# Short-sequence attention on one core: groups of 8 heads with wide PSUM evacuations, a three-stage order written by hand, and casting loads of 16 heads

## The chip, the core and the metric

The kernel runs on one core of a Trainium2 chip. A core has a matrix engine (PE), whose results land in PSUM (8 banks of 2 KB in each of 128 partitions), a vector engine (DVE) and an activation engine (ACT) that read PSUM and write SBUF, a general engine (POOL), a sync engine (SP) and 16 DMA engines that move data between HBM and SBUF. Each engine works through its own instructions in order and waits on semaphores for the others. Here POOL issues the loads and SP the stores. The metric is device time in microseconds (us); lower is better.

## The reference

Softmax attention for 32 batches of 12 heads, each with 128 positions of 64 values, in float32. The 384 heads are independent of each other.

```python
batch, n_heads, seq, head_dim = 32, 12, 128, 64
scale = 1.0 / np.sqrt(q.shape[-1])
scores = scale * np.matmul(q, k.transpose(0, 1, 3, 2))
scores_max = np.max(scores, axis=-1, keepdims=True)
attn = np.exp(scores - scores_max)
attn = attn / (np.sum(attn, axis=-1, keepdims=True) + 1e-8)
return np.matmul(attn, v).astype(np.float32)
```

Both kernels leave out the maximum and divide at the end: the inputs are small, so exp of the plain scores stays in range, and a column of ones beside v gives the sum of each row with the same matmul.

## The kernel before

The loop runs over the 32 batches, and a batch's 12 heads are loaded together. A head's rows lie 256 B long in HBM (64 float32), heads 32 KB apart, so a load of `q_bf` (L52), `k_bf` (L54) or `v_bf` (L57) brings 128 x 12 runs of 256 B and casts them to bf16 on the way. These casting loads are issued by POOL. `v_bf` has a 65th column that POOL sets to 1 (L56). The pool `pbf` has three buffers of each, so a load for batch b+3 waits until batch b's tile has been used.

PE transposes two heads at a time: six transposes of q (L63) and six of k (L70) in a batch, each into a PSUM tile of its own name with one buffer (`qt_ps`, `kt_ps`). ACT copies each `qt_ps` to SBUF (L68), DVE each `kt_ps` (L75). Then, for three groups of four heads: four score matmuls (L84) into `sT_ps`, one PSUM bank a head, single-buffered; one exp of ACT over 128x512 (L92) into `attnT`; and twice two output matmuls (L103) into `o_ps`, single-buffered, each pair copied out by DVE (L110). At the end of a batch DVE takes the reciprocal of the sums (L116), multiplies (L118), and SP stores 384 KB (L119).

The order of the instructions on each engine is set by the tile framework's scheduler, which mixes the transposes of the next batch into the groups of this one; waits for data and buffers are put in by the framework.

Of the kernel before, what the change touches and what calls it, by code (L numbers as in the profile page):

```python
# [1 line left out]

# [5 lines left out]


@with_exitstack
def kernel(
    ctx: ExitStack,
    tc: tile.TileContext,
    q: bass.AP,
    k: bass.AP,
    v: bass.AP,
    out: bass.AP,
):
    nc = tc.nc  # L20
    f32 = mybir.dt.float32
    bf16 = mybir.dt.bfloat16

    B, H, S, D = q.shape
    assert S == 128 and D == 64
    scale = 1.0 / (D ** 0.5)
    HT = 128 // D
    NP = H // HT
    HX = 4
    HO = 2  # L30
    BANK = 512

    qr = q.rearrange("b h s d -> b s h d")
    kr = k.rearrange("b h s d -> b s h d")
    vr = v.rearrange("b h s d -> b s h d")
    orr = out.rearrange("b h s d -> b s h d")

    singles = ctx.enter_context(tc.tile_pool(name="singles", bufs=1))
    ident = singles.tile([128, 128], bf16)
    make_identity(nc, ident)  # L40

    pbf = ctx.enter_context(tc.tile_pool(name="pbf", bufs=3))
    pt = ctx.enter_context(tc.tile_pool(name="pt", bufs=3))
    pa = ctx.enter_context(tc.tile_pool(name="pa", bufs=6))
    po = ctx.enter_context(tc.tile_pool(name="po", bufs=2))
    ps_t = ctx.enter_context(tc.tile_pool(name="ps_t", bufs=1, space=bass.MemoryType.PSUM))
    ps_s = ctx.enter_context(tc.tile_pool(name="ps_s", bufs=1, space=bass.MemoryType.PSUM))
    ps_o = ctx.enter_context(tc.tile_pool(name="ps_o", bufs=1, space=bass.MemoryType.PSUM))

    for b in range(B):  # L50
        q_bf = pbf.tile([128, H, D], bf16, tag="q_bf")
        nc.gpsimd.dma_start(out=q_bf, in_=qr[b])  # L52
        k_bf = pbf.tile([128, H, D], bf16, tag="k_bf")
        nc.gpsimd.dma_start(out=k_bf, in_=kr[b])  # L54
        v_bf = pbf.tile([128, H, D + 1], bf16, tag="v_bf")
        nc.gpsimd.memset(v_bf[:, :, D:D + 1], 1.0)  # L56
        nc.gpsimd.dma_start(out=v_bf[:, :, :D], in_=vr[b])  # L57

        qt = pt.tile([128, NP, 128], bf16, tag="qt")
        kt = pt.tile([128, NP, 128], bf16, tag="kt")  # L60
        for p in range(NP):
            qt_ps = ps_t.tile([128, 128], bf16, tag="qt_ps")
            nc.tensor.transpose(  # L63
                qt_ps,
                q_bf[:, p * HT:(p + 1) * HT, :].rearrange("a b c -> a (b c)"),
                ident,
            )
            nc.scalar.copy(qt[:, p, :], qt_ps)  # L68
            kt_ps = ps_t.tile([128, 128], bf16, tag="kt_ps")
            nc.tensor.transpose(  # L70
                kt_ps,
                k_bf[:, p * HT:(p + 1) * HT, :].rearrange("a b c -> a (b c)"),
                ident,
            )
            nc.vector.tensor_copy(kt[:, p, :], kt_ps)  # L75

        o_b = po.tile([128, H, D + 1], f32, tag="o_b")

        for g in range(H // HX):
            sT_ps = ps_s.tile([128, HX, BANK], f32, tag="sT")  # L80
            for i in range(HX):
                h = g * HX + i
                p, j = divmod(h, HT)
                nc.tensor.matmul(  # L84
                    sT_ps[:, i, :128],
                    lhsT=kt[j * D:(j + 1) * D, p, :],
                    rhs=qt[j * D:(j + 1) * D, p, :],
                    start=True,
                    stop=True,
                )  # L90
            attnT = pa.tile([128, HX, 128], bf16, tag="attnT")
            nc.scalar.activation(  # L92
                out=attnT,
                in_=sT_ps[:, :, :128],
                func=mybir.ActivationFunctionType.Exp,
                bias=0.0,
                scale=scale,
            )
            for gg in range(HX // HO):
                o_ps = ps_o.tile([128, HO, BANK], f32, tag="o_ps")  # L100
                for i in range(HO):
                    h = g * HX + gg * HO + i
                    nc.tensor.matmul(  # L103
                        o_ps[:, i, :D + 1],
                        lhsT=attnT[:, gg * HO + i, :],
                        rhs=v_bf[:, h, :],
                        start=True,
                        stop=True,
                    )
                nc.vector.tensor_copy(  # L110
                    o_b[:, g * HX + gg * HO:g * HX + (gg + 1) * HO, :],
                    o_ps[:, :, :D + 1],
                )

        recip = po.tile([128, H], f32, tag="recip")
        nc.vector.reciprocal(recip, o_b[:, :, D:D + 1])  # L116
        o_sb = po.tile([128, H, D], f32, tag="o_sb")
        nc.vector.tensor_mul(o_sb, o_b[:, :, :D], recip.to_broadcast([128, H, D]))  # L118
        nc.sync.dma_start(out=orr[b], in_=o_sb)  # L119


# [1 line left out]
_INS = ['q', 'k', 'v']  # L123
_OUTS = [((32, 12, 128, 64), 'float32')]


# [23 lines left out]
```

## Time and profile before

| | |
|---|---|
| median of 3 runs | 226.23 us (226.22 to 226.59) |
| span of the profiled execution | 224.4 us |
| instructions | 3513 |
| HBM | 37.75 MB read, 12.58 MB written, 224 GB/s over the span |
| DMA packets | 198,674, of which 198,656 are under 512 B |
| loads, POOL's queue q0 | 148,992 packets, 18.88 MB |
| stores, SP's queue q1 | 49,664 packets, 12.58 MB |
| DMA issues | 32 each of q, k, v (192 KB, 5.1 to 6.4 us to landing) and out (384 KB, 5.7 us) |

The span runs from the first to the last instruction or transfer that the profiler saw; the time of a run has a little more around it. The profiled execution's own time outside the profiler is not listed, so its span stands beside the median. PE is TensorE's matmuls, PEld its weight loads, which lie beside the matmuls. Busy shares are of the span. In the rows by line, what stands behind the first bar is busy time in us and the mean of one instruction in ns, and behind the second the idle time of that engine just before, with what ended it. Rows of waits read: who waited, for whom, us in total, how many times, the longest. A row of the windows view has the stretch, its length, the busy us and count of PE, PEld, DVE, ACT and POOL, the granted PE clock, the DMA share and the GB/s moved, counted by the size that arrives (a load's 256 B in HBM are 128 B in SBUF). Rows of a DMA queue read packets, MB, and the time that the packets took as a share of 16 engines; an engine holds several packets at once, so this goes above 100%. In POOL's timeline a row has its start, duration, line, operation, and in brackets the idle time before.

### The profile page before, as it was taken

The page shows a single profiled execution, that of the slowest core. Times are in us where ns is not written, and L with a number is a line of the kernel's source. Part 1 is how long each engine was busy: PE and PEld are TensorE (multiplying, and loading weights), DVE is VectorE, ACT ScalarE, POOL GpSimd, SP SyncE. Part 2 cuts the span into 40 slices and gives each one's busy share as a digit, 9 for nine tenths or more (in the row PEclk, how much of TensorE's full clock was granted, in tenths as well). Part 3 has the DMA queues.
Part 4 walks back from the last instruction along what each step waited for, and adds up shares of the span by engine and source line. Part 5 has one row for each costly group of instructions (what it writes and reads, how often), then busy time and mean ns, then how long its engine had stood idle before and what let it go on. Part 6 is the DMA issues. An engine that isn't in the chain of part 4 may idle for free.

```text
span 224.4 us, 3513 instructions
## 1 busy us (share of the span) xinstructions
PE 168.3 (75%) x1152; PEld 83.1 (37%) x1152; DVE 120.2 (54%) x448; ACT 99.7 (44%) x289; POOL 101.5 (45%) x134
## 2 busy tenths in 40 slices
PE   0688787788787787877787877788877778878750
PEld 0344333344333343333343333444333334333330
DVE  0264555664555564555564555565555565456652
ACT  2554545445544445444445444444444444444320
POOL 8963455534475443455443455543355534222000
DMA  7999999999999999999999999999999999999333
GB/s 50 149 156 184 148 142 140 155 148 166 151 153 161 161 159 166 148 149 141 129 151 167 146 148 134 137 154 167 149 146 144 135 150 161 142 110 134 76 69 71
DMA packets 198674, 31.69 MB, mean 141 GB/s; under 512 B 198656, under 2 KB 198656, under 8 KB 198656
## 3 DMA queue, kind: packets, MB, share of 16 engines
q0 software_dynamic: 148992, 18.88, 131.9%
q1 hardware_dynamic: 49664, 12.58, 31.0%
q8 instruction: 9, 0.15, 0.3%
q14 instruction: 9, 0.07, 0.1%
HBM read 37.75 MB, written 12.58 MB: 224 GB/s over the span
## 4 chain that ended last, share of the span: by engine, by line
PE 64%; ACT 17%; DVE 9%; issue 6%; DMA 2%; ACTq 0%; POOL 0%; POOLq 0%
PE sT_ps L84 26%; PE qt_ps L63 14%; PE o_ps L103 14%; PE kt_ps L70 11%; ACT attnT L92 9%; ACT qt L68 7%; DVE o_b L110 5%; DVE kt L75 3%; DMA q_bf<-in_q_dram 2%; DVE o_sb L118 1%; ACTq L92 0%; DVE recip L116 0%; POOL ident masks.py:197 0%; POOLq masks.py:199 0%; POOLq L134 0%
## 5 line engine op out<-in xcount | busy, mean ns | idle before, releaser
L68 ACT COPY qt<-qt_ps 128x128 bf16<-128x128 bf16 x192 | 50.4, 263 | 69.0 <-PE qt_ps L63 69.0
L75 DVE COPY kt<-kt_ps 128x128 bf16<-128x128 bf16 x192 | 42.8, 223 | 70.8 <-PE kt_ps L70 66.1
L84 PE MATMUL sT_ps<-qt,kt 64*128 64x128 bf16 x384 | 71.5, 282 | 12.2 <-ACT attnT L92 11.5
L92 ACT ACTIVATE attnT<-sT_ps 128x512 bf16<-128x512 f32 x96 | 57.3, 597 | 47.7 <-PE sT_ps L84 42.9
L63 PE MATMUL qt_ps<-ident,q_bf 128*128 128x128 bf16 x192 | 54.2, 282 | 26.8 <-ACT qt L68 21.4
L110 DVE COPY o_b<-o_ps 128x130 f32<-128x130 f32 x192 | 55.6, 289 | 29.2 <-PE o_ps L103 28.9
L103 PE MATMUL o_ps<-v_bf,attnT 128*128 128x65 bf16 x384 | 56.8, 242 | 6.1 <-DVE o_b L110 6.1
L70 PE MATMUL kt_ps<-ident,k_bf 128*128 128x128 bf16 x192 | 56.4, 294 | 5.3 <-DVE kt L75 4.5
L84 PEld LDWEIGHTS <-kt 64*128 64x128 bf16 x384 | 26.4, 101 | 61.1 <-issue 43.0
L103 PEld LDWEIGHTS <-attnT 128*128 128x128 bf16 x384 | 34.3, 120 | 34.4 <-issue 26.5
L56 POOL MEMSET v_bf<- 128x12 bf16 x32 | 5.0, 155 | 79.9 <-PE o_ps L103 79.9
L52 POOL DMA_DIRECT2D q_bf<-in_q_dram x32 | 32.6, 1020 | 10.2 <-PE qt_ps L63 8.9
L57 POOL DMA_DIRECT2D v_bf<-in_v_dram x32 | 32.6, 1018 | 9.9 <-POOL v_bf L56 9.9
L54 POOL DMA_DIRECT2D k_bf<-in_k_dram x32 | 32.8, 1025 | 1.4 <-PE kt_ps L70 1.4
L63 PEld LDWEIGHTS <-q_bf 128*128 128x128 bf16 x192 | 18.9, 113 | 31.4 <-issue 15.7
L118 DVE TENSOR_TENSOR o_sb<-o_b,recip 128x768 f32<-128x768 f32 x32 | 30.3, 948 | 0.0
L70 PEld LDWEIGHTS <-k_bf 128*128 128x128 bf16 x192 | 23.2, 121 | 8.7 <-issue 0.9
L116 DVE RECIPROCAL recip<-o_b 128x12 f32<-128x12 f32 x32 | 7.0, 219 | 0.0
L68 ACT ACT_TABLE_LOAD x1 | 1.3, 1283 | 0.7 <-PEq L134 0.7
masks.py:199 POOL TENSOR_SCALAR_AFFINE_SELECT ident<-ident 128x128 bf16<-128x128 bf16 x1 | 0.3, 305 | 0.1
masks.py:197 POOL MEMSET ident<- 128x128 bf16 x1 | 0.2, 204 | 0.3 <-POOLq L134 0.3
L134 POOL MEMSET const-float32-0.0<- 128x1 f32 x1 | 0.1, 98 | 0.2 <-issue 0.2
(3 smaller groups left out, 0.3 us busy)
## 6 DMA issues: line engine op xcount, KB each, us to landing
out_dram<-o_sb SPq DMA_DIRECT2D x32, 384.0 KB, 5.7
q_bf<-in_q_dram POOLq DMA_DIRECT2D x32, 192.0 KB, 5.9
k_bf<-in_k_dram POOLq DMA_DIRECT2D x32, 192.0 KB, 6.4
v_bf<-in_v_dram POOLq DMA_DIRECT2D x32, 192.0 KB, 5.1
```

What stands on the lines that cost most here:

```text
L52: nc.gpsimd.dma_start(out=q_bf, in_=qr[b])
L54: nc.gpsimd.dma_start(out=k_bf, in_=kr[b])
L57: nc.gpsimd.dma_start(out=v_bf[:, :, :D], in_=vr[b])
L63: nc.tensor.transpose(qt_ps, q_bf[:, p * HT:(p + 1) * HT, :].rearrange("a b c -> a (b c)"), ident,)
L68: nc.scalar.copy(qt[:, p, :], qt_ps)
L70: nc.tensor.transpose(kt_ps, k_bf[:, p * HT:(p + 1) * HT, :].rearrange("a b c -> a (b c)"), ident,)
L75: nc.vector.tensor_copy(kt[:, p, :], kt_ps)
L84: nc.tensor.matmul(sT_ps[:, i, :128], lhsT=kt[j * D:(j + 1) * D, p, :], rhs=qt[j * D:(j + 1) * D, p, :], start=True, stop=True,)
L92: nc.scalar.activation(out=attnT, in_=sT_ps[:, :, :128], func=mybir.ActivationFunctionType.Exp, bias=0.0, scale=scale,)
L103: nc.tensor.matmul(o_ps[:, i, :D + 1], lhsT=attnT[:, gg * HO + i, :], rhs=v_bf[:, h, :], start=True, stop=True,)
L110: nc.vector.tensor_copy(o_b[:, g * HX + gg * HO:g * HX + (gg + 1) * HO, :], o_ps[:, :, :D + 1],)
L118: nc.vector.tensor_mul(o_sb, o_b[:, :, :D], recip.to_broadcast([128, H, D]))
```

## The change

The batch loop is gone. The 384 heads are one list, cut into 24 chunks of 16 heads for loads and stores and into 48 groups of 8 for compute.

- **Loads.** All 72 loads are issued ahead of everything else in the program, each of 16 heads (2048 runs of 256 B), into 24 buffers of each kind, so none waits for a buffer. The ones beside v are set by DVE.
- **Stage A** of a group: eight transposes (four pairs of q and of k) into one PSUM tile `t_ps` of 1024 bf16, and one DVE copy of all of it. Two buffers.
- **Stage B**: eight score matmuls into `s_ps` (1024 float32, two banks) and one exp over 1024. Even heads lie in the first bank, odd heads in the second. Two buffers.
- **Stage C**: eight output matmuls into `o_ps` (two banks, four heads in each), one buffer; DVE takes the reciprocal and multiplies straight out of PSUM. After each second group SP stores 512 KB.
- **Order**: step s runs A of group s, B of s-1 and C of s-2, as written, not as scheduled.

```diff
-    HX = 4
-    HO = 2
-    BANK = 512
+    CH = 16
+    NCH = N // CH
+    GH = 8
+    NG = N // GH
+    GPC = CH // GH
+    HP = GH // 2
...
+    def heads(x):
+        return x.rearrange("b h s d -> s (b h) d")
...
+    pin = ctx.enter_context(tc.tile_pool(name="pin", bufs=NCH))
+    pt = ctx.enter_context(tc.tile_pool(name="pt", bufs=3))
+    pa = ctx.enter_context(tc.tile_pool(name="pa", bufs=3))
+    po = ctx.enter_context(tc.tile_pool(name="po", bufs=4))
+    ps_t = ctx.enter_context(tc.tile_pool(name="ps_t", bufs=2, space=bass.MemoryType.PSUM))
+    ps_s = ctx.enter_context(tc.tile_pool(name="ps_s", bufs=2, space=bass.MemoryType.PSUM))
+    ps_o = ctx.enter_context(tc.tile_pool(name="ps_o", bufs=1, space=bass.MemoryType.PSUM))
...
-    pbf = ctx.enter_context(tc.tile_pool(name="pbf", bufs=3))
-    pt = ctx.enter_context(tc.tile_pool(name="pt", bufs=3))
-    pa = ctx.enter_context(tc.tile_pool(name="pa", bufs=6))
-    po = ctx.enter_context(tc.tile_pool(name="po", bufs=2))
-    ps_t = ctx.enter_context(tc.tile_pool(name="ps_t", bufs=1, space=bass.MemoryType.PSUM))
-    ps_s = ctx.enter_context(tc.tile_pool(name="ps_s", bufs=1, space=bass.MemoryType.PSUM))
-    ps_o = ctx.enter_context(tc.tile_pool(name="ps_o", bufs=1, space=bass.MemoryType.PSUM))
+    chunks = {}
-    for b in range(B):
...
+    def load(c):
+        sl = slice(c * CH, (c + 1) * CH)
+        q_bf = pin.tile([128, CH, D], bf16, tag="q_bf", name="q_bf")
+        nc.gpsimd.dma_start(out=q_bf, in_=qr[:, sl, :])
+        k_bf = pin.tile([128, CH, D], bf16, tag="k_bf", name="k_bf")
+        nc.gpsimd.dma_start(out=k_bf, in_=kr[:, sl, :])
+        v_bf = pin.tile([128, CH, D + 1], bf16, tag="v_bf", name="v_bf")
+        nc.vector.memset(v_bf[:, :, D:D + 1], 1.0)
+        nc.gpsimd.dma_start(out=v_bf[:, :, :D], in_=vr[:, sl, :])
+        chunks[c] = (q_bf, k_bf, v_bf)
...
+    for c in range(NCH):
+        load(c)
...
+    with tc.manual_schedule():
+        qkts, attns, osbs = {}, {}, {}
...
+        def stage_a(i):
+            c, r = divmod(i, GPC)
+            q_bf, k_bf, v_bf = chunks[c]
+            t_ps = ps_t.tile([128, 2, HP, 128], bf16, tag="t_ps", name="t_ps")
+            for p in range(HP):
+                for j, x in enumerate((q_bf, k_bf)):
+                    h = GH * r + 2 * p
+                    nc.tensor.transpose(
+                        t_ps[:, j, p, :], x[:, h:h + 2, :].rearrange("p h d -> p (h d)"), ident)
+            qkt = pt.tile([128, 2, HP, 128], bf16, tag="qkt", name="qkt")
+            nc.vector.tensor_copy(qkt, t_ps)
+            qkts[i] = qkt
...
+        def stage_b(i):
+            qkt = qkts.pop(i)
+            s_ps = ps_s.tile([128, 2, HP, 128], f32, tag="s_ps", name="s_ps")
+            for p in range(HP):
+                for j in range(2):
+                    pr = slice(j * D, (j + 1) * D)
+                    nc.tensor.matmul(s_ps[:, j, p, :], lhsT=qkt[pr, 1, p, :],
+                                     rhs=qkt[pr, 0, p, :], start=True, stop=True)
+            attn = pa.tile([128, 2, HP, 128], bf16, tag="attn", name="attn")
+            nc.scalar.activation(out=attn, in_=s_ps, func=mybir.ActivationFunctionType.Exp,
+                                 bias=0.0, scale=scale)
+            attns[i] = attn
...
+        def stage_c(i):
+            c, r = divmod(i, GPC)
+            attn = attns.pop(i)
+            v_bf = chunks[c][2]
+            o_ps = ps_o.tile([128, 2, 512], f32, tag="o_ps", name="o_ps")
+            ov = o_ps[:, :, :HP * (D + 1)].rearrange("p j (h e) -> p j h e", h=HP)
+            for h in range(GH):
+                nc.tensor.matmul(ov[:, h // HP, h % HP, :], lhsT=attn[:, h % 2, h // 2, :],
+                                 rhs=v_bf[:, GH * r + h, :], start=True, stop=True)
+            if r == 0:
+                osbs[c] = po.tile([128, CH, D], f32, tag="o_sb", name="o_sb")
+            o_sb = osbs[c]
+            recip = pa.tile([128, 2, HP], f32, tag="recip", name="recip")
+            nc.vector.reciprocal(recip, ov[:, :, :, D])
+            nc.vector.tensor_mul(
+                o_sb[:, GH * r:GH * (r + 1), :].rearrange("p (j h) d -> p j h d", j=2),
+                ov[:, :, :, :D], recip.to_broadcast([128, 2, HP, D]))
+            if r == GPC - 1:
+                nc.sync.dma_start(out=orr[:, c * CH:(c + 1) * CH, :], in_=o_sb)
+                osbs.pop(c)
...
+        for s in range(NG + 2):
+            if s < NG:
+                stage_a(s)
+            if 0 <= s - 1 < NG:
+                stage_b(s - 1)
+            if 0 <= s - 2 < NG:
+                stage_c(s - 2)
```

Three places show how the instructions stand on their engines. In brackets is what an instruction waits for: `PE_49`, `DVE_49`, `Activation_49` and `Pool_49` are the counters of those engines, and `DMASW0_49` to `DMASW7_49` count the loads' landings in eight lanes, so a load that waits for its lane waits for the load eight issues earlier.

POOL in the middle of the program of before, one batch's loads and a half:

```order
L52 DMA q_bf<-in_q_dram 128x12x64 [waits DMASW7_49,PE_49]
L56 MEMSET v_bf 128x12 [waits PE_49]
L57 DMA v_bf<-in_v_dram 128x12x64 [waits DMASW0_49,Pool_49]
L54 DMA k_bf<-in_k_dram 128x12x64 [waits DMASW1_49,PE_49]
L52 DMA q_bf<-in_q_dram 128x12x64 [waits DMASW2_49,PE_49]
```

POOL at the same place of the changed program:

```order
L58 DMA q_bf<-in_q_dram 128x16x64 [waits DMASW1_49]
L60 DMA k_bf<-in_k_dram 128x16x64 [waits DMASW2_49]
L63 DMA v_bf<-in_v_dram 128x16x64 [waits DMASW3_49,DVE_49]
L58 DMA q_bf<-in_q_dram 128x16x64 [waits DMASW4_49]
L60 DMA k_bf<-in_k_dram 128x16x64 [waits DMASW5_49]
```

The waits for PE, which were for a buffer to come free, are gone; the wait of v for DVE is for the column of ones, all of which stand first in DVE's program.

DVE in before, from the end of one batch into the next (the numbers are those of the buffers):

```order
L75 COPY kt_188<-kt_ps_210 128x128 [waits PE_49]
L110 COPY o_b_129<-o_ps_171 128x130 [waits PE_49]
L75 COPY kt_188<-kt_ps_216 128x128 [waits PE_49]
L116 RECIPROCAL recip_175<-o_b_129 128x12 [waits DVE_49]
L110 COPY o_b_225<-o_ps_233 128x130 [waits PE_49]
L118 TENSOR_TENSOR o_sb_177<-o_b_129,recip_175 128x768 [waits DVE_49]
L75 COPY kt_188<-kt_ps_222 128x128 [waits PE_49]
```

DVE in the changed program, two groups of the middle:

```order
L82 COPY qkt_1171<-t_ps_1162 128x1024 [waits PE_49]
L111 RECIPROCAL recip_1193<-o_ps_1184 128x8 [waits PE_49]
L112 TENSOR_TENSOR o_sb_1158<-o_ps_1184,recip_1193 128x512 [waits DVE_49]
L82 COPY qkt_1206<-t_ps_1197 128x1024 [waits PE_49]
L111 RECIPROCAL recip_1229<-o_ps_1219 128x8 [waits PE_49]
L112 TENSOR_TENSOR o_sb_1228<-o_ps_1219,recip_1229 128x512 [waits DMAHW1_49,DVE_49]
```

Fourteen small instructions a batch have become three wide ones a group, and the multiply reads PSUM itself (`DMAHW1_49` counts a store, whose `o_sb` buffer is used again).

PE in before, a piece of the middle in which the next batch's transposes stand among this one's groups:

```order
L84 MATMUL sT_ps_418<-qt_379,kt_380 128x128 [waits Activation_49]
L103 LDWEIGHTS attnT_342
L103 MATMUL o_ps_348<-v_bf_280,attnT_342 128x65 [waits DVE_49]
L103 LDWEIGHTS attnT_342
L103 MATMUL o_ps_348<-v_bf_280,attnT_342 128x65
L84 LDWEIGHTS kt_380
L84 MATMUL sT_ps_418<-qt_379,kt_380 128x128
L63 LDWEIGHTS q_bf_468
L63 MATMUL qt_ps_483<-ident_58,q_bf_468 128x128 [waits Activation_49]
L70 LDWEIGHTS k_bf_374
L70 MATMUL kt_ps_396<-ident_58,k_bf_374 128x128 [waits DVE_49]
```

PE in the changed program, the step in which a new chunk begins; of each run of eight the first rows:

```order
L79 LDWEIGHTS q_bf_105 [waits DMASW1_49]
L79 MATMUL t_ps_427<-ident_79,q_bf_105 128x128
L79 LDWEIGHTS k_bf_107 [waits DMASW2_49]
L79 MATMUL t_ps_427<-ident_79,k_bf_107 128x128
...
L91 LDWEIGHTS qkt_401 [waits DVE_49]
L91 MATMUL s_ps_438<-qkt_401 128x128
...
L105 LDWEIGHTS attn_412 [waits DMASW0_49,DVE_49,Activation_49]
L105 MATMUL o_ps_449<-v_bf_102,attn_412 128x65 [waits PE_49]
```

PE now waits once in eight matmuls, where it waited at nearly every second, and it meets the loads at the head of a chunk: q and k of the new chunk in the transposes, v of the chunk before in the outputs.

More of the change, by code (lines that the diff above doesn't have):

```diff
@@ L26 @@
     scale = 1.0 / (D ** 0.5)
-    HT = 128 // D
-    NP = H // HT
-    HX = 4
-    HO = 2
-    BANK = 512
[L33 to L36, printed above, removed]
-    singles = ctx.enter_context(tc.tile_pool(name="singles", bufs=1))
+    N = B * H
+    CH = 16
[6 more added lines that the diff above has]
+        return x.rearrange("b h s d -> s (b h) d")
@@ new lines @@
+    qr, kr, vr, orr = heads(q), heads(k), heads(v), heads(out)
+    singles = ctx.enter_context(tc.tile_pool(name="singles", bufs=1))
+    pin = ctx.enter_context(tc.tile_pool(name="pin", bufs=NCH))
[4 more added lines that the diff above has]
+    ps_s = ctx.enter_context(tc.tile_pool(name="ps_s", bufs=2, space=bass.MemoryType.PSUM))
@@ L47 @@
-    ps_s = ctx.enter_context(tc.tile_pool(name="ps_s", bufs=1, space=bass.MemoryType.PSUM))
-    ps_o = ctx.enter_context(tc.tile_pool(name="ps_o", bufs=1, space=bass.MemoryType.PSUM))
-    for b in range(B):
[L51 to L119, printed above, removed]
```

## The prediction

> **What bounds the kernel now.** I read the page's busy shares first, then the chain that ended last, then who waited for whom, then the DMA queues.
>
> ```profile
> PE 168.3 (75%) x1152; PEld 83.1 (37%) x1152; DVE 120.2 (54%) x448; ACT 99.7 (44%) x289; POOL 101.5 (45%) x134
> DMA  7999999999999999999999999999999999999333
> PE 64%; ACT 17%; DVE 9%; issue 6%; DMA 2%; ACTq 0%; POOL 0%; POOLq 0%
> ...
> POOL v_bf L56 <- PE o_ps L103: 79.9, 29, 4.2
> ACT qt L68 <- PE qt_ps L63: 69.0, 103, 3.6
> DVE kt L75 <- PE kt_ps L70: 66.1, 95, 7.6
> ...
> PE qt_ps L63 <- ACT qt L68: 21.4, 61, 0.4
> ...
> PE qt_ps L63 <- DMA q_bf<-in_q_dram: 5.3, 1, 5.3
> ```
>
> No engine is full, and the chain passes from PE to ACT and DVE and back: every transpose, score tile and output tile has one PSUM buffer, so PE writes, one small evacuation runs, PE writes again. PE waits for a load once, at the start (5.3 us). The loads wait for PE instead: POOL stands 79.9 us ahead of the v memset until an old v buffer is free. So the compute chain bounds the kernel, at one batch of 12 heads per step. The step is the distance of two rows of POOL's timeline:
>
> ```profile
> 28.31 0.15 POOL L56 MEMSET v_bf<- 128x12 bf16 x1 [3.60 <-PE o_ps L103]
> 28.35 1.01 POOL L52 DMA_DIRECT2D q_bf<-in_q_dram  x1
> ...
> 34.98 0.15 POOL L56 MEMSET v_bf<- 128x12 bf16 x1 [3.60 <-PE o_ps L103]
> ```
>
> 6.67 us a batch, and 32 of them are 213 us of the 224.4 us span. The digits of 9 in the DMA row look like a full DMA, but a digit says only that something was in flight. How close the DMA engines are to their own limit is seen where loads are queued up and nothing else runs. These are the DMA queues for 13 to 19 us, and then five other stretches in this order: 20 to 22, 205 to 207, 33 to 36, 60 to 140 and 219 to 224.4 us.
>
> ```profile
> q0 software_dynamic: 7376, 0.94, 244.3%
> ...
> q1 hardware_dynamic: 1428, 0.36, 85.7%
> q0 software_dynamic: 794, 0.10, 81.5%
> ...
> q0 software_dynamic: 981, 0.12, 102.1%
> q1 hardware_dynamic: 1191, 0.30, 67.6%
> ...
> q0 software_dynamic: 1560, 0.20, 101.8%
> q1 hardware_dynamic: 1399, 0.36, 68.2%
> ...
> DMA packets 75707, 12.07 MB, mean 151 GB/s; under 512 B 75701, under 2 KB 75701, under 8 KB 75701
> ...
> GB/s 0 0 0 0 0 0 0 0 0 0 0 0 0 0 0 0 64 222 220 220 214 216 214 222 220 218 214 218 212 197 40 0 0 0 0 0 0 0 0 0
> ...
> q1 hardware_dynamic: 1552, 0.39, 36.8%
> ```
>
> Loads alone: 7376 packets in 6 us on 16 engines are 13.02 ns per packet and engine, the same through the whole stretch. Over 60 to 140 us it is 80 us x 16 / 75,707 = 16.9 ns. So the steady state of before uses some 77% of what a full queue moves: compute sets the pace now, and the DMA stands close behind it.
>
> **What the change takes from compute.** Each evacuation becomes wide, and each stage works on tiles that were finished one step earlier.
>
> ```profile
> L68 ACT COPY qt<-qt_ps 128x128 bf16<-128x128 bf16 x192 | 50.4, 263 | 69.0 <-PE qt_ps L63 69.0
> L75 DVE COPY kt<-kt_ps 128x128 bf16<-128x128 bf16 x192 | 42.8, 223 | 70.8 <-PE kt_ps L70 66.1
> ...
> L92 ACT ACTIVATE attnT<-sT_ps 128x512 bf16<-128x512 f32 x96 | 57.3, 597 | 47.7 <-PE sT_ps L84 42.9
> ...
> L110 DVE COPY o_b<-o_ps 128x130 f32<-128x130 f32 x192 | 55.6, 289 | 29.2 <-PE o_ps L103 28.9
> ...
> L118 DVE TENSOR_TENSOR o_sb<-o_b,recip 128x768 f32<-128x768 f32 x32 | 30.3, 948 | 0.0
> ...
> L116 DVE RECIPROCAL recip<-o_b 128x12 f32<-128x12 f32 x32 | 7.0, 219 | 0.0
> ```
>
> ACT: 597 - 263 = 334 ns for 384 more elements, 0.87 ns each, so exp over 1024 takes 597 + 512 x 0.87 = 1.04 us, 48 times: 50 us, and the 192 copies are gone. DVE: the 948 ns over 768 elements bound an f32 element by 1.23 ns, so the multiply of 512 takes at most 0.7 us if PSUM adds little; the reciprocal 0.22. The copy of 1024 bf16 isn't in the trace: from the copy of 128 in 223 ns, eight of them bound it above by 1.78 us, and by the o_b copy's 289 ns at 130 f32 a bf16 element is the cheaper one, so I take 0.7 to 1.2. A group of 8 heads costs DVE 1.6 to 2.1 us, 48 groups 77 to 101 us.
>
> PE keeps its 1152 matmuls. Their spacing where PE is dense is bounded by a window of 1 us and a row of the chain:
>
> ```profile
> 13.00:14.00 1.00, 0.98 (x12) 0.66 (x10) 0.50 (x3) 0.54 (x2) 0.00 (x0) 1.00 2.45 156
> ...
> 28.25 0.22 PE sT_ps L84 x2
> ```
>
> 0.082 to 0.11 us each, so 24 per group are 2.0 to 2.6 us. The one single buffer left, o_ps, asks for reciprocal and multiply (0.9 us) between two output stages; transposes and scores of 16 matmuls (1.3 to 1.8 us) stand there in PE's order and cover it. A step of compute is 2.0 to 2.6 us, 16 heads 4 to 5.3 us.
>
> **What it puts in place.** The 72 loads wait for no compute any more, only for the completion of the load eight issues earlier. POOL's 1.01 us per 1536 packets, scaled to 2048, is 1.35 us, less than the 2064 x 13.02 / 16 = 1.68 us that the engines need for it, so up to eight loads stay queued to the end. Three loads are 5.04 us, and with one store of the same 2064 packets 16 heads cost the DMA about 7.1 us. That is above compute's 5.3: **the DMA becomes the bound**, and I price the run as a sum of packets. Wider loads don't make longer packets: each run in HBM stays 256 B. A transfer is its runs and 16 packets more (the 1552 of the last row above are 1536 + 16), so 72 loads and 24 stores of 2064 are 198,144 packets, where before has 128 x 1552 = 198,656.
>
> Start. Rows of the first microseconds:
>
> ```profile
> 2.00:3.00 1.00, 0.00 (x0) 0.00 (x0) 0.00 (x0) 0.02 (x1) 0.91 (x3) 1.00 0.00 0
> 3.00:4.00 1.00, 0.00 (x0) 0.00 (x0) 0.00 (x0) 0.00 (x0) 1.00 (x3) 1.00 1.52 98
> 4.00:5.00 1.00, 0.00 (x0) 0.00 (x0) 0.00 (x0) 0.00 (x0) 1.00 (x2) 1.00 1.84 117
> 5.00:6.00 1.00, 0.35 (x2) 0.19 (x3) 0.00 (x0) 0.27 (x1) 1.00 (x2) 1.00 1.94 125
> 6.00:7.00 1.00, 0.47 (x2) 0.15 (x2) 0.00 (x0) 0.40 (x2) 1.00 (x3) 1.00 2.14 137
> 7.00:8.00 1.00, 0.57 (x4) 0.31 (x3) 0.22 (x1) 0.40 (x2) 1.00 (x3) 1.00 2.24 143
> ```
>
> Packets begin at 3.0 us, and the five slow rows fall short of 156 GB/s by 160 in all, 1.0 us of work: 4.0 us.
>
> Loads: 148,608 packets x 13.02 / 16 = 120.9 us.
>
> Stores beside loads: 22 of 24 (the last two end behind the last load). Their price is what a mixed stretch leaves when its loads are taken at 13.02: (32,000 - 794 x 13.02) / 1428 = 15.2 ns at 20 to 22 us, 16.1 at 205 to 207, 19.8 at 33 to 36. The first two followed a queue that had long been full, as it will be throughout; I take the dearer, 16.1, and keep 13.02 (no dearer than a load) and 19.8 as ends. 22 x 2064 x 16.1 / 16 = 45.7 us, ends 37.0 and 56.2.
>
> Tail. When the last v lands, k has been there for about 2 us and PE has five or six stages left (order: transposes 46, scores 45, outputs 44, and so on). Counted through with 0.082 to 0.11 us a matmul and 0.95 us from outputs to the end of their multiply, the last multiply ends 8.1 to 9.4 us behind k, 5.9 to 7.7 behind v: 6.6. The last store:
>
> ```profile
> 219.34 0.96 DVE L118 TENSOR_TENSOR o_sb<-o_b,recip 128x768 f32<-128x768 f32 x1
> ```
>
> Before it ends at 220.3 and the span at 224.4: 4.1 us, plus 512 more packets alone on the engines (217 GB/s of 256 B are 18.9 ns): 0.6. So 4.7.
>
> Sum: 4.0 + 120.9 + 45.7 + 6.6 + 4.7 = **181.9 us of span**. The median of 226.23 is 1.83 above the profiled span of 224.40; with that, **183.7 us**. DVE's 24 memsets at the start cost nothing here: 0.15 us each by POOL's, under 4 us beside the wait for the first q and k.
>
> [...]
>
> **Rivals.**
>
> *Mixing is dearer than 16.1.* For it: 19.8 at 33 to 36 us, though both queues had work there; at all packets for 16.9, 194,016 x 16.9 / 16 = 204.9 us in place of 166.6, so 222. Against: those stretches follow a queue that had just been short. 194 to 222 us, 14%.
>
> *Compute is the bound after all.* Were the o_ps wait (0.95 us) not covered, a step would be 2.6 + 0.95 = 3.6 us, above the DMA's 3.5: 50 steps, 7 us ahead and 6.5 behind, 193 us. Or PE runs at half speed, as it now idles 2 to 3 us in each 7: 2 x 0.082 x 24 = 3.9 us a step, 210 us. Nothing in the trace shows that: the granted clock is 1.00 in every window, though also in those where PE hasn't begun. Together 6%. [...]
>
> *Slower than before.* Reads and writes of short runs, both queued without a pause, hold each other up at HBM. It decides where a packet costs 17.2 ns ((226.23 - 1.83 - 4.0 - 11.3) x 16 / 194,016). For it: stores alone cost 18.9 ns, and 16.9 is what before averages. At 18.9 for all, 229.2 + 17.1 = 246 us. Against: 2222 packets in the 2 us from 20 are 14.4 ns. 6%.
>
> *Cheaper than 173.* Stores fit between loads at under 13 ns. Nothing shows a packet below 13.02. 4%.
>
> **How the numbers follow.** The forecast, 173 to 194 us by the ends of the store price, has the other 70%. The range of 8 in 10 is 173 to 202: it takes in compute as the bound at 193 and the nearer half of dearer mixing. Faster by over 0.2% (about what a measurement of this kernel can tell from no change) has 92%; 222 us is still faster, so only the last rival and a little of the mixing is left: same 2%, slower 6%.
>
> **What would show it.** Right: loads at 13 ns per packet to within 10 us of the end; PE waiting for DMA of k once per 16 heads, and no longer for ACT or DVE; POOL waiting for DMA; ACT near 50 us and DVE under 105 us. Wrong: PE busy without gaps, or a mixed stretch above 16 ns for most of the run; a flat stretch of loads under 150 GB/s would break the largest term.

## The result, and the profile after

The changed kernel takes **208.44 us** (median of 4 runs, 208.26 to 208.92), the kernel before 226.33 us beside it (4 runs, 226.22 to 226.59): a ratio of 0.9213, 95% interval 0.9200 to 0.9227. It is faster, as forecast, but 25 us above the 183.7 us predicted and above the top of the range, 202.

These are the page's rows that answer to those of before: busy shares, the PE clock and the DMA in 40 slices, the DMA queues, the longest waits, and the costliest groups.

```profile
span 206.5 us, 2823 instructions
...
PE 98.4 (48%) x1152; PEld 72.7 (35%) x1152; DVE 76.2 (37%) x168; ACT 50.3 (24%) x49; POOL 83.0 (40%) x78
...
PEclk9999755558558556655855555557558557555585
DMA  8999999999999999999999999999999999999946
GB/s 51 151 156 156 160 158 157 157 158 157 158 157 159 157 157 158 157 159 158 158 158 158 157 158 157 159 158 158 158 158 157 158 157 159 157 157 158 190 88 128
...
q0 software_dynamic: 148608, 18.88, 142.3%
q1 hardware_dynamic: 49536, 12.58, 44.1%
...
PE t_ps L79 <- DMA q_bf<-in_q_dram: 62.3, 23, 5.8
POOL k_bf L60 <- DMA q_bf<-in_q_dram: 49.4, 18, 3.5
PE t_ps L79 <- DMA k_bf<-in_k_dram: 37.8, 24, 2.9
...
L94 ACT ACTIVATE attn<-s_ps 128x1024 bf16<-128x1024 f32 x48 | 49.0, 1024 | 148.2 <-PE s_ps L91 148.1
L82 DVE COPY qkt<-t_ps 128x1024 bf16<-128x1024 bf16 x48 | 33.2, 691 | 105.2 <-PE t_ps L79 105.2
L112 DVE TENSOR_TENSOR o_sb<-o_ps,recip 128x512 f32<-128x512 f32 x48 | 33.2, 691 | 1.7
```

The bound has moved where the prediction put it. PE, which waited for a load once, now waits 100 us of 206.5 for q and k; POOL waits for loads to land and no longer for PE. The compute terms came out about as written: exp 1.024 us (1.04 forecast), the wide copy 0.69 (0.7 to 1.2), the multiply 0.69 (at most 0.7). But the GB/s row is flat at 158 from start to end. That is the rate of loads alone, in slices where stores of 256 B run beside loads that arrive as 128 B. Stores ought to have lifted it.

What happens there is seen in the queues of a stretch with a store in flight, 45 to 49 us, and of one without, 40 to 42 us:

```profile
q1 hardware_dynamic: 1655, 0.42, 79.9%
q0 software_dynamic: 1655, 0.21, 79.7%
...
q0 software_dynamic: 2461, 0.31, 244.6%
```

Alone, loads run at 2 us x 16 / 2461 = 13.0 ns per packet and engine, as forecast. With a store there is exactly one store packet for each load packet (it holds in each half microsecond too: 207 and 207 in the first), and each takes 4 us x 16 / 3310 = 19.3 ns. If a load packet is still charged its 13.0, a store packet costs **25.7 ns**, where the prediction took 16.1 and an upper end of 19.8. The prediction had named this as a sign of being wrong: a mixed stretch above 16 ns.

The other new row is PEclk: PE was granted the full clock all through before, and 0.621 of it on average here. The prediction had a rival for that, priced at 210 us, close to what was measured. So two causes stand to be told apart, and the runs do it.

### The profile page after: what moved, and what is told of

Same layout as the page of the kernel before. It is cut to its first block, busy times and chain, and to the rows that moved or that the text cites. A ratio compares the mean times of both kernels' runs of the same rounds, so it can differ in the third digit from the quotient of the medians.

```text
span 206.5 us, 2823 instructions
## 1 busy us (share of the span) xinstructions
PE 98.4 (48%) x1152; PEld 72.7 (35%) x1152; DVE 76.2 (37%) x168; ACT 50.3 (24%) x49; POOL 83.0 (40%) x78
## 2 busy tenths in 40 slices
DMA packets 198157, 31.64 MB, mean 153 GB/s; under 512 B 198144, under 2 KB 198144, under 8 KB 198144
## 3 DMA queue, kind: packets, MB, share of 16 engines
q0 software_dynamic: 148608, 18.88, 142.3%
q1 hardware_dynamic: 49536, 12.58, 44.1%
HBM read 37.75 MB, written 12.58 MB: 244 GB/s over the span
## 4 chain that ended last, share of the span: by engine, by line
issue 46%; POOL 39%; DMA 9%; PE 2%; DVE 1%; ACT 1%; POOLq 0%; ACTq 0%
POOL q_bf L58 13%; POOL k_bf L60 13%; POOL v_bf L63 12%; DMA k_bf<-in_k_dram 9%; PE t_ps L79 1%; PE o_ps L105 1%; DVE o_sb L112 1%; ACT attn L94 1%; PE s_ps L91 0%; DVE recip L111 0%; POOLq L63 0%; POOL ident masks.py:199 0%; POOL ident masks.py:197 0%; POOLq masks.py:199 0%; ACTq L94 0%
## 5 line engine op out<-in xcount | busy, mean ns | idle before, releaser
L94 ACT ACTIVATE attn<-s_ps 128x1024 bf16<-128x1024 f32 x48 | 49.0, 1024 | 148.2 <-PE s_ps L91 148.1
L79 PE MATMUL t_ps<-ident,q_bf 128*128 128x128 bf16 x192 | 45.8, 302 | 62.3 <-DMA q_bf<-in_q_dram 62.3
L82 DVE COPY qkt<-t_ps 128x1024 bf16<-128x1024 bf16 x48 | 33.2, 691 | 105.2 <-PE t_ps L79 105.2
L79 PE MATMUL t_ps<-ident,k_bf 128*128 128x128 bf16 x192 | 44.3, 307 | 37.8 <-DMA k_bf<-in_k_dram 37.8
L58 POOL DMA_DIRECT2D q_bf<-in_q_dram x24 | 27.8, 1157 | 30.9 <-issue 30.9
L112 DVE TENSOR_TENSOR o_sb<-o_ps,recip 128x512 f32<-128x512 f32 x48 | 33.2, 691 | 1.7
L105 PE MATMUL o_ps<-v_bf,attn 128*128 128x65 bf16 x384 | 28.1, 235 | 2.1 <-DVE o_sb L112 1.5
L91 PE MATMUL s_ps<-qkt 64*128 64x128 bf16 x384 | 28.3, 297 | 0.0
L105 PEld LDWEIGHTS <-attn 128*128 128x128 bf16 x384 | 20.8, 122 | 11.1 <-issue 8.3
L91 PEld LDWEIGHTS <-qkt 64*128 64x128 bf16 x384 | 16.1, 125 | 9.1 <-issue 8.6
L111 DVE RECIPROCAL recip<-o_ps 128x8 f32<-128x8 f32 x48 | 10.0, 208 | 17.7 <-PE o_ps L105 17.5
## 6 DMA issues: line engine op xcount, KB each, us to landing
v_bf<-in_v_dram POOLq DMA_DIRECT2D x24, 256.0 KB, 18.9
```

Source lines behind the costliest of these rows:

```text
L58: nc.gpsimd.dma_start(out=q_bf, in_=qr[:, sl, :])
L79: nc.tensor.transpose(t_ps[:, j, p, :], x[:, h:h + 2, :].rearrange("p h d -> p (h d)"), ident)
L82: nc.vector.tensor_copy(qkt, t_ps)
L91: nc.tensor.matmul(s_ps[:, j, p, :], lhsT=qkt[pr, 1, p, :], rhs=qkt[pr, 0, p, :], start=True, stop=True)
L94: nc.scalar.activation(out=attn, in_=s_ps, func=mybir.ActivationFunctionType.Exp, bias=0.0, scale=scale)
L105: nc.tensor.matmul(ov[:, h // HP, h % HP, :], lhsT=attn[:, h % 2, h // 2, :], rhs=v_bf[:, GH * r + h, :], start=True, stop=True)
```

## The experiments

Each run starts from the changed kernel, but for the one with deep loads, which starts from the kernel before. Each but the last ran once; the kernel before took 226.2 to 227.3 us on the same chips.

**Without stores.** The store of all chunks but the last is left out:

```diff
             if r == GPC - 1:
-                nc.sync.dma_start(out=orr[:, c * CH:(c + 1) * CH, :], in_=o_sb)
+                if c == NCH - 1:
+                    nc.sync.dma_start(out=orr[:, c * CH:(c + 1) * CH, :], in_=o_sb)
```

> Leaves out 23 of the 24 stores, so all but the last chunk of the output is unwritten. Theory A (load and store packets that take turns on an engine cost 19.4 ns each, so a store packet costs 25.8 beside a load's 13.0): loads run at 13.0 ns per packet to their end, the last lands near 125 us, span 135 to 140 us. Rival B (PE at the halved clock sets the pace, 8.3 us per 16 heads): span stays above 195 us. Rival C (256 B writes to HBM cost what they cost, in whatever company): as A.

Span 136.5 us. The loads run at 13.1 ns per packet (73,422 in the 60 us from 60 on) and compute follows them, so B falls: the same PE work is done in two thirds of the time, with the clock still at 0.76. The 23 stores cost 70.0 us, 3.04 us each, 23.6 ns per packet, though a store alone on the engines took 18.9 ns per packet in the kernel before (256 B at the 217 GB/s of its last store).

**A warm PE.** 36 transposes of the identity are put ahead of each chunk's own:

```diff
+            if r == 0 and c > 0:
+                for _ in range(36):
+                    nc.tensor.transpose(t_ps[:, 0, 0, :], ident, ident)
```

> 36 transposes of the identity ahead of each chunk's first transposes, in the time in which PE waits for q and k, keep PE's clock up. A: clock near 1, span 205 to 208 us, as before this edit. B: span falls by more than 10 us.

The windows of 60 to 80 us, first of the changed kernel, then of this run (behind the five engines stand the clock, the DMA share and the GB/s):

```profile
60.00:80.00 20.00, 10.99 (x127) 8.34 (x127) 7.49 (x15) 5.12 (x5) 8.38 (x8) 0.59 1.97 158
...
60.00:80.00 20.00, 13.15 (x217) 10.94 (x218) 8.28 (x16) 5.72 (x6) 8.27 (x8) 0.91 1.93 158
```

The clock goes from 0.59 to 0.91 in this window (0.87 over the run, where near 1 was expected), the DMA moves the same 158 GB/s, and the span is 207.4. So the halved clock is real and costs nothing here: B has fallen twice.

**Long runs.** The same bytes are stored as 128 runs of 4 KB, to the wrong places of the output:

```diff
+    flat = out.rearrange("b h s d -> (b h s d)").rearrange("(c p f) -> c p f", c=NCH, p=128)
...
-                nc.sync.dma_start(out=orr[:, c * CH:(c + 1) * CH, :], in_=o_sb)
+                nc.sync.dma_start(out=flat[c], in_=o_sb.rearrange("p h d -> p (h d)"))
```

> Each store writes the same 512 KB as 128 runs of 4 KB, to the wrong places of the output; queue and time of issue stay. A: only 144 store packets per chunk take a turn, so a chunk costs the loads' 5.04 us and 1.2 to 1.9 us for the bytes, span 160 to 177 us. B: no change, 206 us. C in the form that the bytes cost it: no change, above 200 us; C in the form that short runs cost it: as A.

Span 165.8 us. Bytes and queue are the same, the store's packets fall from 49,536 to 3,456: a store goes from 3.04 to (165.8 - 136.5) / 23 = 1.27 us (the 1.2 to 1.9 us expected for it was my estimate, with no row of a trace beside it). So the bytes are not what costs. The packets are fewer and longer, and the runs in HBM are longer too; this run doesn't part those.

**One queue.** POOL issues the stores too, between the loads, which now stand four chunks ahead in its program:

```diff
-    for c in range(NCH):
+    AHEAD = 4
+    for c in range(AHEAD):
         load(c)
...
             if r == GPC - 1:
-                nc.sync.dma_start(out=orr[:, c * CH:(c + 1) * CH, :], in_=o_sb)
+                if c + AHEAD < NCH:
+                    load(c + AHEAD)
+                nc.gpsimd.dma_start(out=orr[:, c * CH:(c + 1) * CH, :], in_=o_sb)
```

> Stores go through the loads' own queue (issued by POOL, loads four chunks ahead), so packets no longer alternate between two queues. A: store packets fall to between 13 and 18.9 ns, span 176 to 194 us. B: no change, 206 us. C: no change, 204 to 208 us.

Span 166.4 us, better than A allowed. This row of its page, the sizes of its packets, says why:

```profile
DMA packets 152077, 31.64 MB, mean 190 GB/s; under 512 B 148992, under 2 KB 148992, under 8 KB 152064
```

3,072 packets are of over 2 KB, 128 a store, and the stores' 12.58 MB make them 4 KB each: in this run POOL's queue gathered a partition's 16 runs into one packet. So this run had both edits in one, no second queue and long packets, and doesn't tell them apart. It does show that writing to HBM in runs of 256 B, which by the layout of the output its stores still do, isn't what makes them dear.

**One queue, short packets, first try.** A pad of one element behind each 64 of the output tile was to stop the gathering (the edit is shown against the run with one queue):

```diff
-                osbs[c] = po.tile([128, CH, D], f32, tag="o_sb", name="o_sb")
+                osbs[c] = po.tile([128, CH, D + 1], f32, tag="o_sb", name="o_sb")
...
-                nc.gpsimd.dma_start(out=orr[:, c * CH:(c + 1) * CH, :], in_=o_sb)
+                nc.gpsimd.dma_start(out=orr[:, c * CH:(c + 1) * CH, :], in_=o_sb[:, :, :D])
```

> As the run with one queue, but the output tile in SBUF gets a pad of one element behind each 64, so that a store can't be gathered into 4 KB packets (there 3,072 packets of over 2 KB were seen) and stays 49,152 packets of 256 B. A (taking turns between two queues is dear): no turns in one queue, store packets 13 to 18.9 ns, span 170 to 194 us. C2 (short store packets are dear wherever they are): 25.8 ns as in the changed kernel, span 204 us or more.

Span 166.4 us, with the same 3,072 long packets: it did not make the packets short and tells nothing about them.

**One queue, short packets, second try.** The casting loads are not gathered (148,608 packets for 18.88 MB in the changed kernel), so here the store casts too (the output is rounded to bf16 on the way; again against the run with one queue):

```diff
-                osbs[c] = po.tile([128, CH, D], f32, tag="o_sb", name="o_sb")
+                osbs[c] = po.tile([128, CH, D], bf16, tag="o_sb", name="o_sb")
```

> One queue for loads and stores, with the output tile in bf16 and cast back to float32 by the store, so that its packets should stay single runs as those of the casting loads do (the output is rounded to bf16 on the way). A (taking turns between two queues is dear): no turns, store packets 13 to 18.9 ns, span 171 to 194 us, about 175 if a casting store's packet costs what a casting load's does. C2 (short store packets are dear in any company): 25.8 ns, span 204 us or more. If the packets are gathered into 4 KB again, it tells nothing.

Span 169.9 us, and this time the packets are short. The sizes over the whole run, then those of 60 to 72 us:

```profile
DMA packets 198157, 31.64 MB, mean 186 GB/s; under 512 B 198144, under 2 KB 198144, under 8 KB 198144
...
DMA packets 14936, 2.43 MB, mean 202 GB/s; under 512 B 14935, under 2 KB 14935, under 8 KB 14935
```

12 us x 16 / 14,936 = 12.9 ns is the mean of all packets, loads and stores. The same count of short packets that costs 206.5 us of span in two queues costs 169.9 in one, so C2, which asked for 204 us or more, falls: being short doesn't by itself make a store packet dear. How much of the gain is the missing turns, this run alone can't say. Its store packets read 128 B where the changed kernel's read 256, and they go through POOL's queue: with nothing beside them they take 12.9 to 14.2 ns here (1,236 packets in the microsecond from 158, 1,126 in that from 167), where SP's took 18.9 in the kernel before. Up to 6 of the 12.8 ns between 25.7 and 12.9 may lie there.

**How deep the load queue is.** Two runs made it shorter. First, two buffers of each input in place of 24, with the loads of chunk c + 2 written behind stage C of chunk c; then the same with the ones beside v written by POOL, which stands there until the chunk two before is through (the lines inside `load` belong to the second run alone):

```diff
-    pin = ctx.enter_context(tc.tile_pool(name="pin", bufs=NCH))
+    AHEAD = 2
+    pin = ctx.enter_context(tc.tile_pool(name="pin", bufs=AHEAD))
...
     def load(c):
         sl = slice(c * CH, (c + 1) * CH)
+        v_bf = pin.tile([128, CH, D + 1], bf16, tag="v_bf", name="v_bf")
+        nc.gpsimd.memset(v_bf[:, :, D:D + 1], 1.0)
         q_bf = pin.tile([128, CH, D], bf16, tag="q_bf", name="q_bf")
...
-        v_bf = pin.tile([128, CH, D + 1], bf16, tag="v_bf", name="v_bf")
-        nc.vector.memset(v_bf[:, :, D:D + 1], 1.0)
...
-    for c in range(NCH):
+    for c in range(AHEAD):
...
                 nc.sync.dma_start(out=orr[:, c * CH:(c + 1) * CH, :], in_=o_sb)
                 osbs.pop(c)
+                if c + AHEAD < NCH:
+                    load(c + AHEAD)
```

> Loads may run two chunks ahead and not 24 (two buffers of each kind), so up to five of them are queued where eight were; stores on SP as in the changed kernel. A: turns are taken wherever both queues hold work, mixed stretches stay at 19.4 ns per packet with one load for one store, span 203 to 212 us. D (only a deep load queue takes strict turns): mixed stretches nearer 15 ns, span under 200 us.

> As the run with two buffers, but POOL writes the column of ones and stands there until the chunk two before is through, so at most three or four loads are queued when a store starts, as in the kernel before. A: mixed stretches at 19.4 ns with one load for one store; the DMA also stands idle for 1 to 3 us a chunk, span 215 to 260 us. D: mixed stretches at 14 to 16 ns, in which the loads are held back (fewer than one load packet for a store packet), as at 20 to 22 us of the kernel before; span 195 to 235 us. The packet rates decide, not the span.

The first has a span of 206.0 us, the second (with both edits) 323.2. Their queues in a stretch with a store, 62 to 64 us of the first and 101 to 104 us of the second:

```profile
q0 software_dynamic: 1013, 0.13, 100.2%
q1 hardware_dynamic: 1327, 0.34, 74.7%
...
q1 hardware_dynamic: 1615, 0.41, 75.7%
q0 software_dynamic: 697, 0.09, 45.6%
```

With a short load queue the counts are no longer one for one, and they swing: in the first run from 69 stores and 540 loads in the first half microsecond of this stretch to 522 and 39 in its last. There the packets are cheap, 2 us x 16 / 2340 = 13.7 ns each, which with the load at 13.0 leaves 14.2 for a store packet of 256 B in SP's queue. So neither SP's queue nor two queues at work need be dear. But this is its cheapest stretch: the two microseconds from 70 (1,458 stores and 367 loads) run at 17.5 ns, and stretches of loads alone fall short of a full queue (2,051 packets from 106 to 108 us, where a full one moves 2,461). Over 60 to 140 us the mean packet takes 15.8 ns, against 16.3 in the changed kernel, and the span is no better.

The second run is slower than either theory allowed (A up to 260 us, D up to 235). In each chunk the DMA stands idle: no packet runs from 96.6 to 100.4 us, and PE waits 175 us for q in all. Its packets take 3 us x 16 / 2312 = 20.8 ns, but in the first of these microseconds the store is nearly alone (724 packets, 21 of loads), so it is no fair test of D's price of 14 to 16 ns. In the first run D's price holds in part of the stretches, and D's span under 200 us does not; A's turns of one for one are not seen in either, though no trace shows whether every engine's load queue held a packet all through.

**The kernel before with deep loads.** Only its input buffers go from 3 to 32:

```diff
-    pbf = ctx.enter_context(tc.tile_pool(name="pbf", bufs=3))
+    pbf = ctx.enter_context(tc.tile_pool(name="pbf", bufs=B))
```

> The kernel before with 32 buffers of each input in place of 3, so that its loads run ahead as the changed kernel's do; the order on PE, DVE, ACT and SP is the same. The chain through single PSUM buffers bounds it: 6.67 us per batch stays (the DMA's share of a batch is 3.8 us of loads and at most 2.5 us of stores at 25.8 ns), span 219 to 227 us, and the loads end early in place of keeping pace. Rival (load depth alone makes the gain): span below 212 us.

The span is 224.5 us, as that of before. Its longest waits, and its queues for 62 to 65 us:

```profile
ACT qt L68 <- PE qt_ps L63: 69.3, 103, 3.9
DVE kt L75 <- PE kt_ps L70: 66.3, 95, 7.8
...
q1 hardware_dynamic: 1241, 0.32, 79.8%
q0 software_dynamic: 1241, 0.16, 79.6%
```

Loads that run ahead gain nothing while the chain through single PSUM buffers sets the pace: the gain needs the change's compute. And they alone bring the one-for-one turns at 3 us x 16 / 2482 = 19.3 ns into that kernel, with its 12 heads a store and its old order. Nothing else was edited, so here the full load queue is shown to be what brings the turns and their price.

**A faster version.** The run with one queue (not casting), but the last two chunks' stores go back to SP, where nothing is queued ahead of them, and the last one is split by group:

```diff
-                nc.gpsimd.dma_start(out=orr[:, c * CH:(c + 1) * CH, :], in_=o_sb)
+                if c < NCH - 1:
+                    q = nc.gpsimd if c < NCH - 2 else nc.sync
+                    q.dma_start(out=orr[:, c * CH:(c + 1) * CH, :], in_=o_sb)
                 osbs.pop(c)
+            if c == NCH - 1:
+                h0 = c * CH + GH * r
+                nc.sync.dma_start(out=orr[:, h0:h0 + GH, :], in_=o_sb[:, GH * r:GH * (r + 1), :])
```

> One queue for loads and stores, with the last two chunks' stores back on SP and the last one split by group. A: 164 to 167 us of time, a ratio to before of 0.73 to 0.74, against 168.2 of the run with one queue.

167.03 us (4 runs, 166.91 to 167.15), a ratio of 0.738 to the kernel before, 95% interval 0.7368 to 0.7393: the gain of the change is 18 us, that of moving the stores into POOL's queue, where they are also gathered, another 41. That is just above the 164 to 167 us expected.

## Why the prediction was right in kind and wrong in size

- **What bounded before: right.** The run with 32 buffers shows it: no wait for a buffer, no change of time.
- **The compute terms: right, or a little dear.** ACT 50.3 us busy (50 forecast), DVE 76.2 (77 to 101). A step of compute, between two rows of scores in PE's timeline of the changed kernel, is 1.94 us, just under the 2.0 to 2.6 forecast, and that at a granted clock of 0.50:

```profile
61.22 0.61 PE L91 MATMUL s_ps<-qkt 64*128 64x128 bf16 x8
...
63.16 0.61 PE L91 MATMUL s_ps<-qkt 64*128 64x128 bf16 x8
```

- **The loads, 120.9 us: right.** 13.0 ns per packet against 13.02, where nothing else ran.
- **The stores, 45.7 us: the step that failed.** The price of a store packet beside loads was 16.1 ns and measured 25.7. This row is the stores' queue from 0 to 193 us, when the last loads are about to land:

```profile
q1 hardware_dynamic: 43344, 11.01, 43.3%
```

  That is 21 stores of 2064, one fewer than the 22 I had put beside loads. 21 x 2064 x 25.7 / 16 = 69.6 us, 23.9 more than the term, of the 24.6 us by which the span missed. I had taken the price from 20 to 22 and 205 to 207 us of before, as stretches that "followed a queue that had long been full". Their rows spoke against it: 1428 stores for 794 loads and 1191 for 981 are not one for one, so they showed the pattern of a short load queue, and the first was about to run short. The row that I set aside, 33 to 36 us with 1399 for 1560, looks nearest to what the change brings, but only in its total: by half microseconds it swings from 388 stores and 109 loads to 110 and 413. No stretch of before that I read had the steady turns, so none could give their price. Filling the load queue to eight, which the change does on purpose, is what made the stores dear. The rival "mixing is dearer" (194 to 222 us, 14%) was what happened, though its reason, stretches behind a queue that had just been short, was not: the full queue did it.
- **The range.** Its top at 202 cut that rival in half. With 25.7 ns for 21 stores the sum would have been 207.6 us, against 208.4 measured.
- **The tail: near.** From k of the last chunk (193.88 us) to the last multiply's end (201.6) 7.7 us, a little under the 8.1 to 9.4; from there 4.9 to the end, against 4.7.
- **The clock: wrong, without effect.** Against a fall I had the granted clock of 1.00 in every window of before. PE's timeline of the changed kernel around one wait:

```profile
63.70 0.46 PE L105 MATMUL o_ps<-v_bf,attn 128*128 128x65 bf16 x8
...
66.67 0.23 PE L79 MATMUL t_ps<-ident,q_bf 128*128 128x128 bf16 x1 [2.51 <-DMA q_bf<-in_q_dram]
...
69.27 0.29 PE L79 MATMUL t_ps<-ident,k_bf 128*128 128x128 bf16 x1 [2.37 <-DMA k_bf<-in_k_dram]
```

  PE waits for q, does a single transpose, and waits again for k: 5 us in which it does one matmul, and the granted clock, the third number from the end of these rows, falls from 1.00 to 0.50:

```profile
64.00:67.00 3.00, 0.39 (x6) 0.13 (x3) 0.90 (x2) 0.89 (x1) 0.24 (x2) 1.00 1.92 160
68.00:73.00 5.00, 3.73 (x47) 2.95 (x47) 2.20 (x4) 1.23 (x2) 2.36 (x3) 0.50 1.82 158
```

  The fall came with waits of 2.51 and 2.37 us and one matmul between them, and the warm run, which puts transposes into such waits, stood at 0.91 where this kernel stood at 0.59 (60 to 80 us); how much idle time a fall takes, no run shows. What the rival had wrong is that this would set the pace: it priced a step at 3.9 us by doubling 0.082 us a matmul, and at clock 0.50 a step takes 1.94, less than half of the 4.2 us that the DMA takes for a group (5.04 us of loads and 3.3 of stores per chunk, halved). That its 210 us lay near the measured time was chance, as the warm run shows.
- **The price of a short packet: not one number.** Loads alone took 13.0 ns, and all packets of the run with casting stores in one queue 12.9; where two queues take turns a packet takes half as much again (19.3), and SP's stores alone took 18.9. With the deep load queue the counts were one for one (1655 to 1655); with two buffers they swung (69 stores and 540 loads, then 522 and 39), and no trace shows whether a queue was empty at times.

What stays open: why a pair of one load and one store packet costs some 13 ns more in turns than in one queue, how much of that is SP's store packet itself, and which condition besides the load queue's depth decides whether the turns are strict. No run separates these. The shares in the rows do show where the time goes: share x time x 16 / count is how long one packet is under way. Loads alone, that is 31.8 ns with 2.4 packets at once on an engine; in turns the load packet still takes 30.8 ns and the store packet 30.9, but only 1.6 are under way at once. In the cheap stretch of the shorter queue a store packet took 18.0.

## What to carry to other kernels

When a change turns a compute-bound kernel into a DMA-bound one, price its transfers from a stretch in which the queues stand to each other as they will afterwards; where one queue's packets are to meet another's, look at the ratio of the two counts before using the rate. Short store packets beside a deep queue of short load packets cost here about double what a load packet does (25.7 against 13.0 ns); try them in the loads' own queue, or make them long. And before calling a low clock the cause, see whether the engine waits for something else anyway.

## What the runs showed of the hardware that was not expected

- Two queues that both have short packets took strict turns in both kernels whose loads were eight deep (1655 to 1655, and 1241 to 1241), at 19.3 ns a packet against a mean of 12.9 in one queue (with casting stores).
- POOL's queue gathered the 16 runs of a partition into one 4 KB packet when a store didn't cast (3,072 such packets in 24 stores), with or without a pad in SBUF; SP's queue sent each run as its own packet of 256 B (49,536 packets for 12.58 MB), and a casting transfer in POOL's queue was not gathered either (198,144 of 198,157 packets under 512 B). With gathered packets a chunk takes 6.46 us (POOL's issues of q at 62.20 and 68.66 us in the run with one queue), of which the loads are 5.04 and a 512 KB store 1.42:

```profile
62.20 1.14 POOL L58 DMA_DIRECT2D q_bf<-in_q_dram  x1 [0.49 <-issue]
...
68.66 1.14 POOL L58 DMA_DIRECT2D q_bf<-in_q_dram  x1 [0.49 <-issue]
```

- POOL's issue of a load of 2064 packets takes 1.14 us, not the 1.35 that scaling by packets from 1.01 us gave.
